# Moving a bias product, eight sums and the last SwiGLU to later or earlier places in the tail of a mixture-of-experts decoder layer

## The chip, the cores and the metric

The kernel runs on one core of one Trainium2 chip. The metric is the device time of one execution in microseconds (us). Engines are named as in the profile: PE (TensorE, matmuls), PEld (its weight loads), DVE (VectorE), ACT (ScalarE), POOL (GpSimd), SP (SyncE, which here issues the large transfers).

## The reference

One post-norm decoder layer over 512 tokens of width 1024: a mixer (a convolution group and dilated attention heads, both projected), a layer norm, a mixture of 32 experts with the top 4 of each token, and a second layer norm. The change lies in the second half:

```python
def reference(...):
    mix = hybrid_mixer(x, ...)
    x = layer_norm(ALPHA * x + mix, ln1_g, ln1_b)
    ffn = moe_ffn(x, router_w, router_b, w_gate, b_gate, w_up, b_up, w_down, b_down)
    return layer_norm(ALPHA * x + ffn, ln2_g, ln2_b)
...
def expert_block(xb, e):                      # one block of tokens that chose expert e
    g = jnp.minimum(xb @ w_gate[e] + b_gate[e], 7.0)
    u = jnp.clip(xb @ w_up[e] + b_up[e], -7.0, 7.0)
    hdn = (u + 1.0) * g * jax.nn.sigmoid(1.702 * g)
    return hdn @ w_down[e] + b_down[e]        # weighted by the gate, added to the token's row
```

## The kernel before, in words

The front (mixer, first norm, routing) fills the first 270 us or so. After it the 32 experts are worked through in an order that is fixed by hand. A *position* is a place in that order, 0 to 31. Tokens of an expert lie in blocks of 32; four blocks make a group. Position 29 has two blocks, positions 30 and 31 have one each, and the one block of position 31 is a group by itself.

For each position `expert` (L1072 to L1128) does on PE four gate/up chunks (L1081 the gate and up biases, L1084 the products), then two down chunks (L1110, L1113). Weights arrive in 2 MB pieces in a ring of seven buffers; a piece is loaded again as soon as PE has read it. After the fourth gate/up chunk comes `swiglu` (L1058): DVE makes `gm` and `um` from PSUM, ACT makes the sigmoid `sg`, DVE multiplies twice and transposes into `hT`, which the down products need. After the down products ACT and DVE copy the result out of PSUM in a high and a low part (`wh`/`yh` L1126, `yl` L1128).

`combine` (L1141) adds finished groups to the tokens' rows `acc`: it makes a one-hot matrix `cg` on DVE (L1146), and then eight times a sum on PE (L1154) and an add on DVE (L1155). Its pieces stand in a list `combs`; `fill` takes the next piece of the oldest entry. `tick(c)` is called after chunk c of a position (0 to 3 gate/up, 4 and 5 down) and calls `fill` as often as `FILLS`, or in the last positions a tuple of its own, says. So `combs` and these numbers set what PE does between chunks. The one-hot is the first piece that `fill` takes of an entry.

`add_bias` (L1325) is an entry of the same list: PE transposes the gates (L1332), DVE copies them (`cg`, L1333), eight PE products with the table of down biases (L1339: 32 rows of the table against 512 columns) are added to `acc` on DVE (L1341), and four PE products with one row (L1346) spread the second norm's gain and bias over the partitions, which ACT copies (L1347).

`overflow` (L1359) is a short entry too: four small PE products and some sixteen small DVE instructions that count blocks over the planned capacity.

Position 31 has its own `tick`: all that is left in `combs` at chunk 0 (`ENDC`), and pieces of `outputs` (L1434) by `ENDO`. A piece of `outputs` works on 128 tokens: statistics on DVE (L1429, L1430), square root (L1431) and scaling (L1446) on ACT, and one step later the gain on DVE (L1449), the bias on POOL (L1451) and the store. Five such pieces make the four row blocks; the sixth (L1457) picks the last group's rows for `last_rows` (L1467), which finishes them when the last down product is there and sends them off with an indirect store (L1563).

Of the kernel before, what the change touches and what calls it, by code (L numbers as in the profile page):

```python
# [18 lines left out]
T, D, H, E, NE, TOPK = 512, 1024, 8, 64, 32, 4  # L19
# [68 lines left out]
LOOK = 2  # L88

FILLS = {False: (0, 0, 0, 3, 0, 0), True: (2, 2, 0, 0, 0, 0)}  # L90
ENDC, ENDO = (99, 99, 99, 99, 0, 0), (0, 3, 2, 6, 0, 0)

PTAPS, GTAPS = (0,) * 4, (8,) * 4
LAGS = dict(V=1.0, bias=-28556.5, c0=30039.3, c1=30045.5, c2=-28570.8, c3=-29890.6, conv0=-29716.5, conv1=30103.6,
# [171 lines left out]
def tile_layer(ctx: ExitStack, tc: tile.TileContext, x, positions, w_in, conv_w, conv_b, conv_ln_g,  # L266
# [792 lines left out]
    def swiglu(st, r, ps):  # L1059
# [10 lines left out]
        V.transpose(st["hT"][:, r].rearrange("p b t -> p (b t)"), um)  # L1070

    def expert(tag, rows, sel, tick, pool=(gd, "gd"), small=lambda: None, keep=False):  # L1072

        ps = [pool[0].tile([128, 2, 256], F32, name=pool[1]) for _ in rows]
        bv = bT.rearrange("p g (h q j) -> p g h q j", h=2, q=4)
        for c in range(4):
            w = got[tag, "gu", c].rearrange("p g k (h q j) -> p k g h q j", h=2, q=4)
            for i, (st, r) in enumerate(rows):
                if c == 0:
                    for q in range(4):  # L1080
                        P.matmul(ps[i][q * 32:(q + 1) * 32], sel[0:96], bv[:, :, :, q], start=True, stop=False)  # L1081
                for k in range(2):
                    for q in range(4):
                        P.matmul(ps[i][q * 32:(q + 1) * 32], st["xT"][:, r, c * 2 + k], w[:, k, :, :, q], start=False,  # L1084
                                 stop=(c == 3 and k == 1))
                if c:
                    small()
                if c == 3:
                    swiglu(st, r, ps[i])
            advance()  # L1090
            tick(c)
# [10 lines left out]
        for c in range(2):  # L1102
            w = got[tag, "dn", c].rearrange("p k (b q c) -> p k q b c", b=4, q=4)
            for u_, (st, r, n) in enumerate(units):
                d = ds_[u_]
                for k in range(4):
                    kw = dict(start=(c == 0 and k == 0), stop=(c == 1 and k == 3))
                    for j in range(4):
                        if n == 2:
                            P.matmul(d[j * 32:(j + 1) * 32], st["hT"][:, r + j % 2, c * 4 + k],  # L1110
                                     w[:, k, 2 * (j // 2):2 * (j // 2) + 2], **kw)
                        else:
                            P.matmul(d[j * 32:(j + 1) * 32, 0:256], st["hT"][:, r, c * 4 + k], w[:, k, j], **kw)  # L1113
            advance()
            tick(4 + c)
# [16 lines left out]
    def place_y(st):  # L1132

        g = st["g"]
        while any(g - 3 in c[1] for c in combs):
            fill()
        if g % 3 not in ys:
            ys[g % 3] = px.tile([128, D], F32R, name="wh" if g % 3 < 2 else "wl")
        st["yh"], st["yl"] = ys[g % 3], mw.tile([128, D], F32R, name="yl", bufs=3)

    def combine(sts):  # L1141

        parts = []
        for st in sts:
            cg = mw.tile([128, T], F32R, name="cg")
            V.tensor_scalar(cg, iota1, st["tk"][:, 0:1], None, op0=OP.is_equal)  # L1146
            parts += [(cg, st[y], st["used"] * 32) for y in ("yh", "yl")]
        yield
        for tt in range(TT):
            for hf in range(2):  # L1150
                c = slice(hf * 512, (hf + 1) * 512)
                ps = cb.tile([128, 512], F32, name="cb")
                for j, (cg, y, n) in enumerate(parts):
                    P.matmul(ps, cg[0:n, tt * 128:(tt + 1) * 128], y[0:n, c], start=(j == 0), stop=(j == len(parts) - 1))  # L1154
                V.tensor_tensor(acc[:, tt, c], acc[:, tt, c], ps, OP.add)  # L1155
                yield
# [33 lines left out]
    GS, combs = {}, []  # L1190

    def begin(i):

        return [(g, s_) for g in range(len(GS), last_group(i) + 1)
                for s_ in [slots(members[g], lambda p, tt: rk1[:, tt, p:p + 1], lambda p, tt: aux[:, tt, p])]
                if next(s_, 0) is None]

    def middle(new):
        for g, s_ in new:
            next(s_)  # L1200

    def finish(new):
        for g, s_ in new:
            GS[g] = dict(next(s_), g=g)

    def ready_x(n):
        for g in range(n + 1):
            if "xT" not in GS[g]:
                xpose(GS[g])

    def fill():
        while combs:
            combs[0][2] -= 1
            if next(combs[0][0], 0) is None:
                return
            combs.pop(0)

    def last_group(i):
        return order[min(i, NE - 1)][1][-1][0]
# [106 lines left out]
    def add_bias():  # L1326

        t = got["last"]
        GT = mw.tile([128, T], F32, name="cg")
        ps = cb.tile([128, 512], F32, name="cb")  # L1330
        for tt in range(TT):
            P.transpose(ps[0:NE, tt * 128:(tt + 1) * 128], Gf[:, tt], ident)  # L1332
        V.tensor_copy(GT[0:NE], ps[0:NE])  # L1333
        bdp = t[0:NE, 0].rearrange("p (b q c) -> p q b c", b=4, q=4)
        yield
        for tt in range(TT):
            for hf in range(2):
                ps = cb.tile([128, 512], F32, name="cb")
                P.matmul(ps, GT[0:NE, tt * 128:(tt + 1) * 128], bdp[:, 2 * hf:2 * hf + 2], start=True, stop=True)  # L1339
                c = slice(hf * 512, (hf + 1) * 512)  # L1340
                V.tensor_tensor(acc[:, tt, c], acc[:, tt, c], ps, OP.add)  # L1341
            yield
        for i in range(4):
            c = slice(i % 2 * 512, (i % 2 + 1) * 512)
            ps = cb.tile([128, 512], F32, name="cb")
            P.matmul(ps, one1, t[0:1, 2 + i // 2, c], start=True, stop=True)  # L1346
            S.activation(t[:, i // 2, c], ps, AF.Copy)  # L1347
            if i % 2:
                yield
# [9 lines left out]
    def overflow():  # L1359

        pcs = cb.tile([128, 512], F32, name="cb")
        for tt in range(TT):
            P.matmul(pcs[:, 0:NE], onesb, mp[:, tt], start=(tt == 0), stop=(tt == TT - 1))
        V.tensor_tensor(ov[:, 0], pcs[:, 0:NE], cap, OP.subtract)
        V.tensor_scalar(ov[:, 1], ov[:, 0], 0.0, None, op0=OP.is_gt)
        for r in range(1, 4):
            V.scalar_tensor_tensor(ov[:, 1], ov[:, 0], 128.0 * r, ov[:, 1], op0=OP.is_gt, op1=OP.add)

        V.tensor_copy(ov[:, 2], ov[:, 1])
        for sft in (1, 2, 4, 8, 16):  # L1370
            V.tensor_copy(ov[:, 3], ov[:, 2])
            V.tensor_tensor(ov[:, 2, sft:NE], ov[:, 3, sft:NE], ov[:, 3, 0:NE - sft], OP.add)
        V.tensor_tensor(ov[:, 1], ov[:, 2], ov[:, 1], OP.subtract)
        V.tensor_copy(nit, ov[0:1, 2, NE - 1:NE])
        yield
# [114 lines left out]
    for i, (p, rows) in enumerate(order):  # L1490
        def tick(c):

            if c == 0:
                middle(new)
            if c == 0 and i == 1:
                combs.append([overflow(), (), 9])
            if c == 1:
                finish(new)
                new.clear()
            if c == 4:  # L1500
                ready_x(last_group(i + 1))
            if c == 5:
                new.extend(begin(i + 1 + LOOK))
            fills = FILLS[len(rows) > 2] if i < NE - 3 else (3, 3, 3, 3, 3, 3)
            if c == 0 and combs and combs[0][1] and combs[0][2] == 9:

                fill()
            if c < 2 and any(g - 3 in k[1] for k in combs for g, r in rows if "yh" not in GS[g]):

                for _ in range(min(3, combs[0][2] - sum(fills[c:]))):  # L1510
                    fill()
            for _ in range(fills[c]):
                fill()

        if i + 1 < NE:
            expert(p, [(GS[g], r) for g, r in rows], selr[:, p] if p else sel0, tick, small=lambda: next(first, 0))
        else:
            break
        if i == LASTC:
            combs.append([add_bias(), (), 9])  # L1520

        ready = order[i + 1][1][0][0] if i + 1 < NE - 1 else ngrp - 1
        while done < ready:
            n = 2 if done < ngrp - 3 else 1
            if done + n > ready:
                break
            combs.append([combine([GS[g] for g in range(done, done + n)]), range(done, done + n), 9])
            done += n

# [61 lines left out]
```

## Time and profile before

| what | us |
|---|---|
| median of 3 runs (lowest, highest) | 1302.81 (1300.8, 1302.96) |
| the profiled execution: its own time | 1306.11 |
| the profiled execution: span of the core | 1304.4 |
| PE busy (share of the span) | 1227.5 (94%) |
| PEld, DVE, ACT, POOL busy | 581.5, 606.1, 280.4, 185.3 |
| moved by the DMA engines | 441.94 MB, 339 GB/s |

The own time is 1.7 us more than the span, which counts from the first to the last instruction. Rows of the trace give times from the start of the span. Time before and time of the profiled execution differ by 3.3 us, so that sums over rows fit the profiled execution and not the median.

### The profile page before, as it was taken

What the parts mean: (1) busy time and instruction counts of PE and PEld (TensorE: products, weight loads), DVE (VectorE), ACT (ScalarE), POOL (GpSimd) and SP (SyncE); (2) the same over time, 40 slices, a digit from 0 to 9 for tenths busy, and PEclk for the clock granted to TensorE, in tenths of its full rate; (3) what the DMA queues carried; (4) which work ended last, traced back from release to release, by engine and by line L of the source; (5) the groups of instructions that cost most, each with busy time, mean ns of one, the idle gap of its engine ahead of it and who ended that gap; (6) DMA issues with size and microseconds to landing.
All of it is one profiled execution on the core that took longest, in us unless ns stands there. A gap on an engine that the chain in (4) does not pass through costs nothing. (4 is left out here: it accounts for less than half of the span.)

```text
span 1304.4 us, 25419 instructions
## 1 busy us (share of the span) xinstructions
PE 1227.5 (94%) x10578; PEld 581.5 (45%) x10578; DVE 606.1 (46%) x1444; ACT 280.4 (21%) x551; POOL 185.3 (14%) x158
## 2 busy tenths in 40 slices
PE   8989999889899999999999899999999999999984
PEld 7767767623233343343344334343435334533332
DVE  6999855743433333342333423344234444324464
ACT  5677782311000010010010001110101110101122
POOL 2854101312011011011001110001101101000002
PEclk9999999879899999999999999999999999999877
DMA  9400324679999999999999999999999999899781
GB/s 293 160 1 1 129 82 173 242 279 377 420 420 419 422 419 421 423 415 419 422 419 420 417 419 422 414 405 419 419 421 410 419 422 419 320 351 368 304 362 68
DMA packets 68658, 441.94 MB, mean 339 GB/s; under 512 B 8279, under 2 KB 16615, under 8 KB 27580
## 3 DMA queue, kind: packets, MB, share of 16 engines
q1 hardware_dynamic: 64748, 429.98, 81.6%
q0 software_dynamic: 3792, 10.29, 2.3%
q8 instruction: 85, 1.39, 0.4%
q14 instruction: 33, 0.27, 0.1%
HBM read 435.99 MB, written 4.33 MB: 338 GB/s over the span
## 5 line engine op out<-in xcount | busy, mean ns | idle before, releaser
L1084 PE MATMUL gd<-wt,xTg 128*32 128x512 f32 x4304 | 505.9, 599 | 7.4 <-DMA wt<-in_exp_w_up_dram 5.1
L1084 PEld LDWEIGHTS gd<-wt,xTg 128*32 128x32 f32 x4304 | 158.2, 111 | 288.2 <-issue 268.4
L1110 PE MATMUL gd<-wt,hT 128*32 128x512 f32 x1472 | 192.4, 602 | 15.3 <-DVE hT L1070 12.6
L1020 POOL DMA_INDIRECT xg<-x1d,idx x78 | 74.4, 954 | 864.7 <-DVE tk L1049 820.8
L1066 ACT ACTIVATE sg<-gm 128x256 f32<-128x256 f32 x78 | 32.5, 417 | 618.1 <-DVE gm L1065 616.0
L1065 DVE TENSOR_SCALAR gm<-gd 128x256 f32<-128x256 f32 x77 | 30.9, 402 | 217.1 <-PE gd L1084 211.0
L1128 DVE TENSOR_TENSOR yl<-gd,wh 32x256 fp32r<-32x256 f32 (+1 forms) x104 | 53.4, 513 | 143.3 <-ACT wh L1126 142.3
L1110 PEld LDWEIGHTS gd<-wt,hT 128*32 128x32 f32 x1472 | 58.6, 111 | 130.3 <-issue 95.7
L1126 ACT ACTIVATE wh<-gd 32x256 fp32r<-32x256 f32 (+1 forms) x104 | 46.8, 450 | 195.0 <-PE gd L1110 135.2
L548 PE MATMUL bk<-wt,wh 128*128 128x512 f32 (+1 forms) x352 | 81.2, 378 | 1.4 <-ACT sg L592 0.7
L1155 DVE TENSOR_TENSOR acc<-acc,cb 128x512 f32<-128x512 f32 x88 | 57.6, 678 | 49.9 <-PE cb L1154 49.7
L1113 PE MATMUL gd<-wt,hT 128*32 128x256 f32 x1056 | 73.0, 392 | 4.6 <-issue 2.5
L1084 PE MATMUL gd<-wb,xTg 128*32 128x512 f32 x624 | 76.7, 593 | 0.0
L548 PEld LDWEIGHTS bk<-wt,wh 128*128 128x128 f32 x352 | 61.1, 188 | 14.7 <-ACT sg L592 1.4
L586 DVE SCALAR_TENSOR_TENSOR bk<-u,cT,bk 128x512 f32<-128x512 f32 x88 | 66.2, 753 | 1.8
L1154 PE MATMUL cb<-yl,cg 128*128 128x512 f32 (+2 forms) x160 | 64.7, 404 | 0.0
L1113 PEld LDWEIGHTS gd<-wt,hT 128*32 128x32 f32 x1056 | 42.4, 113 | 32.6 <-issue 15.5
L1154 PE MATMUL cb<-wh,cg 128*128 128x512 f32 (+2 forms) x112 | 48.2, 431 | 5.9 <-DVE cg L1146 5.9
L1081 PE MATMUL gd<-wl,selr 96*32 96x512 bf16 x296 | 49.1, 385 | 0.0
L548 PE MATMUL bk<-wt,wl 128*128 128x512 f32 (+1 forms) x176 | 41.7, 379 | 2.5 <-DVE wl L539 2.1
L1069 DVE SCALAR_TENSOR_TENSOR um<-um,tk,sg 128x256 f32<-128x256 f32 x78 | 39.7, 509 | 8.9
L1128 DVE TENSOR_TENSOR yl<-gd,wl 64x512 fp32r<-64x512 f32 (+1 forms) x36 | 20.5, 570 | 48.8 <-ACT wl L1126 48.5
(340 smaller groups left out, 1292.6 us busy)
## 6 DMA issues: line engine op xcount, KB each, us to landing
wt<-in_exp_w_gate_dram SPq DMA_DIRECT2D x112, 1024.0 KB
wt<-in_exp_w_up_dram SPq DMA_DIRECT2D x112, 1024.0 KB
wt<-in_exp_w_down_dram SPq DMA_DIRECT2D x52, 2048.0 KB
wb<-in_exp_w_down_dram SPq DMA_DIRECT2D x12, 2048.0 KB
wb<-in_exp_w_gate_dram SPq DMA_DIRECT2D x16, 1024.0 KB
wb<-in_exp_w_up_dram SPq DMA_DIRECT2D x16, 1024.0 KB
wt<-in_w_in_dram SPq DMA_DIRECT2D x3, 2048.0 KB
acc<-in_x_dram SPq DMA_DIRECT2D x8, 512.0 KB
```

Of the source, the lines that this page charges most:

```text
L548: P.matmul(b.t[:, ts], w.t[:, k], xx[:, k, ts], start=(pas == 0 and k == 0), stop=(pas == 2 and k == KT - 1))
L586: op("V", 0.663, (lambda j: lambda e: V.scalar_tensor_tensor(b.t, u[:, c, j:j + T], cT[:, c, j:j + 1], b.t, op0=OP.mult, op1=OP.add))(j), ...
L1020: G.indirect_dma_start(out=xg[:, r], out_offset=None, in_=x1d[:, :], in_offset=bass.IndirectOffsetOnAxis(ap=idx[:, r:r + 1], axis=0))
L1069: V.scalar_tensor_tensor(um, um, st["tk"][:, 8 + r:9 + r], sg, op0=OP.mult, op1=OP.mult)
L1081: P.matmul(ps[i][q * 32:(q + 1) * 32], sel[0:96], bv[:, :, :, q], start=True, stop=False)
L1084: P.matmul(ps[i][q * 32:(q + 1) * 32], st["xT"][:, r, c * 2 + k], w[:, k, :, :, q], start=False, stop=(c == 3 and k == 1))
L1110: P.matmul(d[j * 32:(j + 1) * 32], st["hT"][:, r + j % 2, c * 4 + k], w[:, k, 2 * (j // 2):2 * (j // 2) + 2], **kw)
L1113: P.matmul(d[j * 32:(j + 1) * 32, 0:256], st["hT"][:, r, c * 4 + k], w[:, k, j], **kw)
L1126: S.activation(st["yh"][o], a, AF.Copy)
L1128: V.tensor_tensor(st["yl"][o], a, st["yh"][o].bitcast(F32), OP.subtract)
L1154: P.matmul(ps, cg[0:n, tt * 128:(tt + 1) * 128], y[0:n, c], start=(j == 0), stop=(j == len(parts) - 1))
L1155: V.tensor_tensor(acc[:, tt, c], acc[:, tt, c], ps, OP.add)
```

## The change

A new function `prime` makes the one-hot of the oldest entry of `combs` as soon as that entry is the oldest, at the end of a position or in `fill`, and not at the first `fill` of the next position. `overflow` no longer stands in the list: its pieces are issued together after chunk 4 of position 1. `add_bias` is put in with a count that keeps `prime` off it. The many fills (18 a position) now belong to position 30 alone; position 29 takes `FILLS`, three after chunk 3. In position 31 `ENDO` leaves the third and later pieces of `outputs` but one until after `swiglu`.

```diff
-ENDC, ENDO = (99, 99, 99, 99, 0, 0), (0, 3, 2, 6, 0, 0)
+ENDC, ENDO = (99, 99, 99, 99, 0, 0), (0, 2, 1, 6, 0, 0)
...
     def fill():
         while combs:
+            prime()
             combs[0][2] -= 1
             if next(combs[0][0], 0) is None:
+                if not combs[0][2]:
+                    combs.pop(0)
+                    prime()
                 return
             combs.pop(0)
+
+    def prime():
+
+        if combs and combs[0][2] == 9:
+            combs[0][2] = 8
+            next(combs[0][0])
...
-            if c == 0 and i == 1:
-                combs.append([overflow(), (), 9])
+            if c == 4 and i == 1:
+                for _ in overflow():
+                    pass
...
-            fills = FILLS[len(rows) > 2] if i < NE - 3 else (3, 3, 3, 3, 3, 3)
-            if c == 0 and combs and combs[0][1] and combs[0][2] == 9:
-
-                fill()
+            fills = FILLS[len(rows) > 2] if i < NE - 2 else (2, 3, 3, 3, 3, 2)
...
         if i == LASTC:
-            combs.append([add_bias(), (), 9])
+            combs.append([add_bias(), (), 99])
...
             done += n
+        prime()
```

The instructions of PE and DVE are the same set before and after, but for two more rows on DVE where a run of adds is cut; on ACT a load of the sigmoid's and square root's tables changes place; POOL and SP keep their order. Lines from `prime` on have numbers that are 8 to 10 higher after the change (L1332 becomes L1342, L1339 L1349, L1346 L1356, L1449 L1459).

First place, PE. Before, the bias products stand in position 29 (`x16` is a gate/up chunk of two blocks):

```order
L1332 MATMUL cb<-cst,Gf 32x128 x4
L1339 MATMUL cb<-wt_70,cg 128x512 x2
L1084 MATMUL gd<-wt_1842,xTg 32x512 x16
L1339 MATMUL cb<-wt_70,cg 128x512 x6
L1084 MATMUL gd<-wt_1922,xTg 32x512 x16
L1346 MATMUL cb<-wt_70,one_2115 128x512 x4
L1113 MATMUL gd<-wt_1979,hT 32x256 x32
```

After, they stand in position 30, whose chunks have one block (`x8`); the sums of the last shared group come behind them:

```order
L1084 MATMUL gd<-wt_71,xTg 32x512 x8
L1342 MATMUL cb<-cst,Gf 32x128 x4
L1349 MATMUL cb<-wt_70,cg 128x512 x2
L1084 MATMUL gd<-wt_1789,xTg 32x512 x8
L1349 MATMUL cb<-wt_70,cg 128x512 x6
L1084 MATMUL gd<-wt_1842,xTg 32x512 x8
L1356 MATMUL cb<-wt_70,one_2115 128x512 x4
L1154 MATMUL cb<-wh,cg 128x512
L1154 MATMUL cb<-yl,cg 128x512
L1084 MATMUL gd<-wt_1922,xTg 32x512 x8
```

The products with 32 rows and with one row have kept their order but stand between shorter chunks. In position 29 four sums are left after chunk 0 and twelve stand after chunk 3.

Second place, DVE at the start of position 30. Before:

```order
L1128 TENSOR_TENSOR yl<-gd,wh 32x256 x8
L1146 TENSOR_SCALAR cg<-cst,tk 128x512
L1155 TENSOR_TENSOR acc<-acc,cb 128x512 x8
L1065 TENSOR_SCALAR gm<-gd 128x256
L1067 TENSOR_SCALAR um<-gd 128x256
```

After:

```order
L1128 TENSOR_TENSOR yl<-gd,wh 32x256 x8
L1343 COPY cg<-cb 32x512
L1351 TENSOR_TENSOR acc<-acc,cb 128x512 x8
L1146 TENSOR_SCALAR cg<-cst,tk 128x512
L1155 TENSOR_TENSOR acc<-acc,cb 128x512
L1065 TENSOR_SCALAR gm<-gd 128x256
```

Behind the eight `yl` now stands the copy of the transposed gates, where the one-hot stood.

Third place, DVE in position 31. Before:

```order
L1449 TENSOR_TENSOR yl<-xg,wt_70 128x4x4x64
L1429 BN_STATS lst<-acc 128x6 x2
L1430 BN_AGGR lst<-lst 128x2
L1443 RECIPROCAL lst<-lst 128x1
L1444 TENSOR_SCALAR lst<-lst 128x1
L1449 TENSOR_TENSOR xTg<-xg,wt_70 128x4x4x64
L1449 TENSOR_TENSOR hT<-xg,wt_70 128x4x4x64
L1065 TENSOR_SCALAR gm<-sl 128x256
L1067 TENSOR_SCALAR um<-sl 128x256
L1068 SCALAR_TENSOR_TENSOR um<-um,gm 128x256
L1069 SCALAR_TENSOR_TENSOR um<-um,tk,sg 128x256
L1070 STREAM_TRANSPOSE hT<-um 128x256
```

After:

```order
L1459 TENSOR_TENSOR yl<-xg,wt_70 128x4x4x64
L1065 TENSOR_SCALAR gm<-sl 128x256
L1067 TENSOR_SCALAR um<-sl 128x256
L1068 SCALAR_TENSOR_TENSOR um<-um,gm 128x256
L1069 SCALAR_TENSOR_TENSOR um<-um,tk,sg 128x256
L1070 STREAM_TRANSPOSE hT<-um 128x256
L1439 BN_STATS lst<-acc 128x6 x2
L1440 BN_AGGR lst<-lst 128x2
L1453 RECIPROCAL lst<-lst 128x1
L1454 TENSOR_SCALAR lst<-lst 128x1
L1459 TENSOR_TENSOR xTg<-xg,wt_70 128x4x4x64
L1459 TENSOR_TENSOR hT<-xg,wt_70 128x4x4x64
```

The five instructions of the last SwiGLU have passed the fourth block's statistics and the gains of the third and fourth block.

## Rows read from the trace of the kernel before

**Rows 1.** A window: busy PE, PEld, DVE, ACT, POOL, clock, DMA share, GB/s.
```profile
1200.00:1225.00 25.00, 24.07 (x156) 9.06 (x158) 11.27 (x23) 3.22 (x6) 0.95 (x1) 0.93 0.76 289
```

**Rows 2.** Timeline of PE, 1000 to 1100 us: start, length, work, idle before.
```profile
1068.72 2.50 PE L1084 MATMUL gd<-wt,xTg 128*32 128x512 f32 x16 [2.51 <-DMA wt<-in_exp_w_up_dram]
```

**Rows 3.** Timeline of PE, position 29.
```profile
1192.99 0.50 PE L1154 MATMUL cb<-wh,cg 128*128 128x512 f32 x1
...
1195.96 3.64 PE L1084 MATMUL gd<-wt,xTg 128*32 128x512 f32 x32
...
1200.58 0.60 PE L1332 MATMUL cb<-cst,Gf 128*32 128x128 f32 x4
1202.11 1.98 PE L1339 MATMUL cb<-wt,cg 32*128 32x512 f32 x4 [0.93 <-DVE cg L1333]
1204.02 3.64 PE L1084 MATMUL gd<-wt,xTg 128*32 128x512 f32 x32
1207.59 5.41 PE L1339 MATMUL cb<-wt,cg 32*128 32x512 f32 x12
1212.93 5.34 PE L1084 MATMUL gd<-wt,xTg 128*32 128x512 f32 x32
1218.20 3.69 PE L1346 MATMUL cb<-wt,one 1*128 1x512 f32 x8
```

**Rows 4.** Timeline of PE, positions 30 and 31.
```profile
1228.76 0.40 PE L1081 MATMUL gd<-wl,selr 96*32 96x512 bf16 x4
...
1232.85 0.47 PE L1154 MATMUL cb<-wh,cg 128*128 128x512 f32 x1 [1.98 <-DVE cg L1146]
...
1246.82 3.10 PE L1113 MATMUL gd<-wt,hT 128*32 128x256 f32 x32 [2.47 <-issue]
...
1256.99 0.47 PE L1154 MATMUL cb<-wh,cg 64*128 64x512 f32 x1 [2.88 <-DVE cg L1146]
...
1263.50 7.52 PE L1084 MATMUL sl<-wt,xTg 128*32 128x512 f32 x48
...
1283.87 3.64 PE L1113 MATMUL sl<-wt,hT 128*32 128x256 f32 x32 [5.33 <-issue]
```

**Rows 5.** Windows of 3 us, columns as in rows 1.
```profile
1209.00:1212.00 3.00, 3.00 (x9) 1.29 (x8) 2.49 (x4) 0.00 (x0) 0.00 (x0) 1.00 0.79 309
1212.00:1215.00 3.00, 3.00 (x15) 0.77 (x17) 1.38 (x3) 0.00 (x0) 0.00 (x0) 0.72 0.80 320
...
1233.00:1236.00 3.00, 3.00 (x14) 1.41 (x18) 1.97 (x3) 0.00 (x0) 0.00 (x0) 0.63 1.02 437
...
1248.00:1251.00 3.00, 3.00 (x36) 1.95 (x32) 0.00 (x0) 0.00 (x0) 0.00 (x0) 0.53 1.00 418
...
1260.00:1263.00 3.00, 3.00 (x9) 2.24 (x7) 2.34 (x5) 0.00 (x0) 0.00 (x0) 0.50 0.99 421
```

**Rows 6.** Timeline of DVE, position 1 and positions 30 and 31.
```profile
341.56 1.39 DVE L1128 TENSOR_TENSOR yl<-gd,wh 64x512 fp32r<-64x512 f32 x2 [7.68 <-ACT wh L1126]
...
1228.86 3.46 DVE L1128 TENSOR_TENSOR yl<-gd,wh 32x256 fp32r<-32x256 f32 x8 [8.06 <-ACT wh L1126]
...
1255.54 0.68 DVE L1537 TENSOR_SCALAR ohl<-cst,rk 128x32 f32<-128x32 f32 x4
...
1256.38 0.47 DVE L1146 TENSOR_SCALAR cg<-cst,tk 128x512 fp32r<-128x512 f32 x1
...
1271.98 1.53 DVE L1449 TENSOR_TENSOR yl<-xg,wt 128x1024 f32<-128x1024 f32 x1
...
1278.24 0.42 DVE L1065 TENSOR_SCALAR gm<-sl 128x256 f32<-128x256 f32 x1
...
1279.02 1.78 DVE L1068 SCALAR_TENSOR_TENSOR um<-um,gm 128x256 f32<-128x256 f32 x1
...
1289.86 0.42 DVE L1471 TENSOR_TENSOR wt<-wt,sl 128x256 f32<-128x256 f32 x1 [6.09 <-PE sl L1113]
```

**Rows 7.** Timeline of POOL, position 31.
```profile
1273.66 2.35 POOL L1451 TENSOR_TENSOR yl<-yl,wt 128x1024 f32<-128x1024 f32 x1 [1.22 <-DVE yl L1449]
1277.24 3.29 POOL L1451 TENSOR_TENSOR xTg<-xTg,wt 128x1024 f32<-128x1024 f32 x1 [1.23 <-DVE xTg L1449]
```

## The prediction

> **What bounds the kernel now.** I first asked where time can still be won. Until about 1070 us it is the weights: the timeline of PE shows its last wait for them, 2.51 us at 1068.72 [rows 2]. What is saved ahead of that point is waited for again there, as long as it is no more than 2.51. After it the weights are early: in 1200 to 1225 the DMA engines are busy 0.76 of the time while PE works 24.07 of 25 us [rows 1]. So the tail is bound by PE, and there every wait of PE and every loss of its clock shows in the end. The timeline of PE has these waits: 0.93 for the copy of the gates in position 29 [rows 3], 1.98 and 2.88 for a one-hot, 2.47 and 5.33 for a SwiGLU [rows 4]. [...] From the first row block on the chain runs on DVE: the last SwiGLU starts only at 1278.24, though the last gate/up chunk ended at 1271.02 [rows 4, 6].
>
> **The change part by part.** *One-hots earlier, overflow later.* Before 1068 nothing is won [rows 2]. `overflow` has DVE to itself, since DVE sits idle 7.68 us before the `yl` at 341.56 [rows 6]; moved behind one down chunk, its sixteen instructions still fit at the some 0.2 us that such small ones take, which I estimate as under half of the 0.42 of a `gm` [rows 6]. Without that cover it would cost about 3 us, ahead of 1068. I count 0.
>
> *Position 29* loses the transposes, the wait and the first products (1200.58 to 1204.02, 3.44), the others (1207.59 to 1212.93, 5.34), the one-row products (3.69) and the slow chunk's loss (5.34 less the 3.64 of an undisturbed one, 1.70): **14.2** [rows 3]. Its sums stay, twelve of them behind chunk 3. They take 2.97 (1192.99 to 1195.96) and so cover the SwiGLU, whose wait in position 30 is 2.47 [rows 3, 4]. Position 30 then begins at 1214.6 instead of 1228.76.
>
> *Position 30* gets the bias work: transposes 0.60, eight products 1.98 + 5.41 less the overlap of neighbours, 7.3, one-row products 3.69: 11.6 at the full clock [rows 3]. The wait for the one-hot does not vanish. It becomes one for the copy of the gates, which on DVE stands behind the same eight `yl`: these end 3.56 after the position's start (1228.86 + 3.46 against 1228.76), the copy adds up to 0.93, so PE goes on after 4.4; it has worked 2.1 (1232.85 less the wait of 1.98) and 0.6, and waits 1.7 [rows 3, 4, 6]. That is 0.3 less. Six sums in front of the down products cover half of 2.97, so 1.5, of the 2.47. Together 11.6 - 0.3 - 1.5 = **9.8** more.
>
> *Position 31*: the one-hot passes the four `ohl` and two small instructions (1255.54 to 1256.38, 0.84), and one sum pair, 0.5, now fills part of the wait [rows 6, 4]. So its first sum comes 14.2 - 9.8 + 0.84 + 0.5 = **5.7** earlier than 1256.99, at the same loss of clock.
>
> *The clock* is the open price. Position 30 before has two falls; each costs what the slow chunk lost, 1.7, so 3.4 [rows 3, 5]. After, there lies between the copy and the last gate/up chunk a stretch of 7.3 + 3.7 of 32-row and one-row products, three chunks of 1.9 (half of 3.64 and a little) and a sum pair: 17 us at the full clock [rows 3]. [...] Below: one fall, as after the same products before, 1.7, which is 1.7 better than now. Above: the clock stays down throughout, 17, which is 13.6 worse. The row nearest to it is 1260 to 1263: narrow sums on a busy PE, and the clock stays at 0.50; the three chunks behind them took 7.52 where 5.7 would do, so it comes back late [rows 4, 5]. In position 29 the chunks between the narrow products were 3.64 long, here they are half of that. I take two thirds of the stretch, 11, hence 11 - 3.4 = **7.6** worse. That is the choice on which the number depends most.
>
> [...]
>
> *The last SwiGLU.* On DVE it now follows the second block's gain, which ends at 1273.51 (1271.98 + 1.53) [rows 6]. Not all of 1278.24 - 1273.51 = 4.7 is plain to see: POOL's add of that block runs 1273.66 to 1276.01 [rows 7], and the SwiGLU's first product with two operands in SBUF took 1.78 at 1279.02 and ended at 1280.80, just behind POOL's 1280.53, so it waits for POOL [rows 6, 7]. After, it would start at 1274.3 and end at 1276.3. The other two instructions take about two fifths of 2.47, 1.0, so that `hT` is there at 1277.3 and the down products start at 1277.4 instead of 1283.87, 6.4 earlier [rows 4]. What is late next is the rest of the row blocks, which is now behind the SwiGLU. On DVE it is the 4.7 between 1273.51 and 1278.24, so it would end at 1277.3 + 4.7 = 1282.0; and as the third gain is over before the fourth block is scaled, POOL can take its turn of 2.35 in between, which makes 1284.4 [rows 6, 7]. The down products, if they take the 6.0 they took (1283.87 to 1289.86), end at 1283.4, before that. So the last rows begin at 1284.4 instead of 1289.86: **5.4** earlier [rows 4, 6]. Bounds: 6.4 if the row blocks don't stand in the way, 3.1 if POOL holds DVE for one more turn of 2.35.
>
> *Sum* against the profiled execution: 5.7 - 7.6 + 5.4 = **3.5**. Its own time 1306.11 becomes 1302.6. The median is 3.3 below that execution, and I take the same difference off: **1299.3**.
>
> **The rivals.** *The clock mostly stays up.* Then the stretch costs 1.7 to 7 and the gain, which is 5.7 + 5.4 + 3.4 = 14.5 less the stretch's loss, is 12.8 to 7.5, so 1290.0 to 1295.3. For it: the chunks between are wide and each fall so far ended with such work. Against: the busy PE at 0.50 in 1260 to 1263 [rows 5]. [...]
>
> *Nothing that can be measured*, 1300.3 to 1305.3: the clock costs 12 to 17, and the move of the bias work takes back what the SwiGLU gives. For it: the products of 32 rows and of one row are 11 of 17 us, and at half the clock they last 22. Here the change moves the bias work without its waits going, and only the end gains.
>
> [...]
>
> **How the numbers follow.** What a measurement of this kernel can tell from no change is about 0.2%, 2.6 us: faster is below 1300.2, slower above 1305.4. Chances: forecast, 1296 to 1300.2, 0.36; clock up 0.16; nothing measurable 0.29; slower 0.19. So faster 0.52, same 0.29, slower 0.19. The range leaves out the best part of the first rival and most of the slower one: 1291.5 to 1306.0. The forecast's own range is 1296 to 1302.
>
> **What would show it.** Position 30 starts 14 us earlier and is 10 to 17 us longer. PE waits about 1.7 us there behind L1343's copy. The granted clock between the bias products is near 0.5 for most of the stretch; a clock near 1 is the first rival. The last SwiGLU starts right behind the second block's gain, its first product in SBUF is held by POOL to some 2 us after its start, and the wait of 5.33 before the last down products shrinks below 2. The last rows start behind the fourth block's gain on DVE and not behind PE. The forecast is wrong if the clock holds, or if DVE and POOL hold each other for longer than 5 us in the last position.

## The result, and the profile after

The changed kernel takes **1296.21 us** (median of 5, 1292.78 to 1298.51) against 1302.96 (median of 5 beside it): ratio 0.9933, 95% interval 0.9909 to 0.9958. Twelve more executions on another chip (an experiment below) gave 1300.73 against 1304.76, ratio 0.9967 (0.9946 to 0.9987). So it is faster, by 4 to 7 us; forecast were 3.5 us and 1299.3. The two profiled executions differ by more than that, 1304.4 to 1294.2 in span, and the rows show why.

PE after, from position 29 on (start, length, work, idle before and what ended it):

```profile
1187.59 0.50 PE L1154 MATMUL cb<-wh,cg 128*128 128x512 f32 x1
...
1209.28 0.40 PE L1081 MATMUL gd<-wl,selr 96*32 96x512 bf16 x4
...
1213.59 1.98 PE L1349 MATMUL cb<-wt,cg 32*128 32x512 f32 x4 [1.65 <-DVE cg L1343]
1215.49 1.92 PE L1084 MATMUL gd<-wt,xTg 128*32 128x512 f32 x16
1217.35 7.67 PE L1349 MATMUL cb<-wt,cg 32*128 32x512 f32 x12
1224.95 3.64 PE L1084 MATMUL gd<-wt,xTg 128*32 128x512 f32 x16
1228.52 7.19 PE L1356 MATMUL cb<-wt,one 1*128 1x512 f32 x8
...
1242.86 1.93 PE L1113 MATMUL gd<-wt,hT 128*32 128x256 f32 x32 [0.63 <-DVE hT L1070]
...
1252.26 0.47 PE L1154 MATMUL cb<-wh,cg 64*128 64x512 f32 x1 [1.30 <-DVE cg L1146]
...
1272.39 1.93 PE L1113 MATMUL sl<-wt,hT 128*32 128x256 f32 x32
```

Beside [rows 3, 4]: position 29's first sum starts at 1187.59 instead of 1192.99, so 5.40 us were there before the tail began. Position 29 takes 21.69 (to 1209.28) instead of 35.77. From there to the last group's first sum it is 42.98 instead of 28.23. A gate/up chunk of one block (x16) takes 1.92 at 1215.49, and the next one 3.64 at 1224.95: that is the clock, as the windows after say (the number behind the busy times and ahead of the DMA share is the granted clock):

```profile
1216.00:1219.00 3.00, 3.00 (x20) 1.06 (x13) 0.78 (x2) 0.00 (x0) 0.00 (x0) 1.00 1.01 421
1219.00:1222.00 3.00, 3.00 (x6) 1.21 (x5) 1.92 (x4) 0.00 (x0) 0.00 (x0) 0.72 0.95 404
1222.00:1225.00 3.00, 3.00 (x8) 0.70 (x9) 1.02 (x2) 0.00 (x0) 0.00 (x0) 0.50 0.99 412
...
1237.00:1240.00 3.00, 3.00 (x16) 0.40 (x8) 0.59 (x1) 0.00 (x0) 0.00 (x0) 0.50 0.05 19
1240.00:1243.00 3.00, 2.37 (x14) 1.40 (x14) 2.31 (x6) 0.42 (x1) 0.00 (x0) 0.86 0.48 123
```

In this execution PE is busy 3.00 of 3.00 when the clock falls, and it stands at 0.50 from about 1220 to 1241, through the bias work and one chunk more. A second trace of the same kernel, shown below, has the fall at another place.

DVE and then POOL after, position 31:

```profile
1266.40 1.53 DVE L1459 TENSOR_TENSOR yl<-xg,wt 128x1024 f32<-128x1024 f32 x1
1267.86 0.41 DVE L1065 TENSOR_SCALAR gm<-sl 128x256 f32<-128x256 f32 x1
...
1268.64 2.08 DVE L1068 SCALAR_TENSOR_TENSOR um<-um,gm 128x256 f32<-128x256 f32 x1
...
1275.36 3.28 DVE L1459 TENSOR_TENSOR hT<-xg,wt 128x1024 f32<-128x1024 f32 x1 [0.24 <-ACT xg L1456]
1278.56 0.41 DVE L1481 TENSOR_TENSOR wt<-wt,sl 128x256 f32<-128x256 f32 x1
```

```profile
1268.09 2.35 POOL L1461 TENSOR_TENSOR yl<-yl,wt 128x1024 f32<-128x1024 f32 x1 [1.23 <-DVE yl L1459]
1275.20 2.35 POOL L1461 TENSOR_TENSOR xTg<-xTg,wt 128x1024 f32<-128x1024 f32 x1 [4.76 <-DVE xTg L1459]
...
1285.95 0.89 POOL L1572 DMA_INDIRECT out_dram<-wt,ti  x1 [4.88 <-issue]
```

The SwiGLU starts right behind the second gain, its first product with both operands in SBUF ends just after POOL's add (1268.09 to 1270.44) and takes 2.08 where the median of this line is 0.42, the down products start without a wait at 1272.39, and the last rows start behind the fourth gain, which took 3.28 beside POOL's next add (1275.20 to 1277.55) where the second took 1.53. From the last group's first sum to the last rows it is 26.30 instead of 32.87 [rows 4, 6]. From the last rows to the end it is 15.64 instead of 14.54.

So the 10.2 us between the two profiles are -5.40 ahead of position 29, -14.08 in it, +14.75 to the last group's first sum, -6.57 to the last rows, +1.10 to the end. The tail alone gives 4.8.

### The profile page after: what moved, and what is told of

It is laid out like the page before. It is cut to its first block, busy times and chain, and to the rows that moved or that the text cites. A ratio compares the mean times of both kernels' runs of the same rounds, so it can differ in the third digit from the quotient of the medians.

```text
span 1294.2 us, 25413 instructions
## 1 busy us (share of the span) xinstructions
PE 1227.4 (95%) x10578; PEld 581.2 (45%) x10578; DVE 605.7 (47%) x1444; ACT 280.5 (22%) x551; POOL 184.0 (14%) x158
```

## The experiments

Each was timed beside the kernel before on its chip: the first four on one, the next four on a second, three on a third and the last by itself.

| kernel | us | kernel before | ratio (95%) |
|---|---|---|---|
| the SwiGLU's place alone | 1301.02 | 1304.89 | 0.997 (0.9952 to 0.9987) |
| all but the SwiGLU's place | 1300.06 | 1304.89 | 0.997 (0.9953 to 0.9988) |
| one-hots and overflow alone | 1303.03 | 1304.89 | 0.9984 (0.9963 to 1.0005) |
| after, bias products on 128 rows | 1289.84 | 1304.89 | 0.99 (0.9878 to 0.9921) |
| after, gain and bias spread by DMA | 1293.63 | 1304.76 | 0.9904 (0.9879 to 0.993) |
| after, both | 1287.7 | 1304.76 | 0.9861 (0.9835 to 0.9887) |
| after, bias back in position 29 | 1300.5 | 1304.76 | 0.9968 (0.9955 to 0.9981) |
| after, again | 1300.73 | 1304.76 | 0.9967 (0.9946 to 0.9987) |
| both, bias back in position 29 | 1293.01 | 1302.95 | 0.9912 (0.989 to 0.9934) |
| both, again | 1285.43 | 1302.95 | 0.9856 (0.9833 to 0.988) |
| both, old places of output rows | 1290.19 | 1302.95 | 0.9892 (0.9869 to 0.9915) |
| both, without the last store | 1287.26 | 1306.18 | 0.986 (0.9811 to 0.9909) |

**The parts of the change alone.** The kernel before with the new `ENDO`:

```diff
-ENDC, ENDO = (99, 99, 99, 99, 0, 0), (0, 3, 2, 6, 0, 0)
+ENDC, ENDO = (99, 99, 99, 99, 0, 0), (0, 2, 1, 6, 0, 0)
```

> The kernel before with the order of the output pieces in position 31 alone changed, so that the last SwiGLU passes the third and fourth block. If it is worth what the prediction's sum gave, about 5.4 us less than before, 1297.5; in its profile the last down products start at most 2 us after PE's warm-up matmuls, and all ahead of the second block's gain is as before. If the row blocks merely take the place of the SwiGLU at the end, within 1.5 us of before.

The changed kernel with the old `ENDO`, the same line the other way round:

> The changed kernel with the old order of output pieces in position 31, so that only the move of the bias work, the sums and the one-hots is left. By the prediction's sum (5.7 - 7.6 for the tail, nothing ahead of it) 1.9 us slower than before, 1304.9; if waits ahead of the tail count after all, or the clock holds more often than not, 1.4 us or more faster than before, 1301.5 or less, which with e1 would add up to the change's 6.75.

The changed kernel with the old `ENDO` and the old fills, so that of the change only the earlier one-hots and the place of `overflow` are left:

```diff
-            fills = FILLS[len(rows) > 2] if i < NE - 2 else (2, 3, 3, 3, 3, 2)
+            fills = FILLS[len(rows) > 2] if i < NE - 3 else (3, 3, 3, 3, 3, 3)
```

> The kernel before with one-hots made early and overflow out of the list, the bias work left in position 29 and the old order of output pieces. By the theory that waits ahead of 1068 us are made good by the weights, only the tail's waits count: 1.98 and 0.84 go and with the first its fall of the clock, 2.8 to 4.5 less than before, 1298.5 to 1300.2, with position 29 starting within 1 us of before. By the rival that each wait of PE counts, two more waits of 1.0 go and position 29 starts 2 us or more earlier, 5 to 6.5 less, 1296.5 to 1298.

Measured: 3.9, 4.8 and 1.9 us less than before. The first two are together 0.6% by their ratios, where the change itself gave 0.67% and 0.33%; with some 0.2% of noise on each, that fits, but says no more. The second is a miss: without the SwiGLU's place the prediction's sum gave a loss of 1.9 us, and 4.8 were gained. The third is not told from zero. In its trace the wait of 1.98 in position 30 stayed where I had expected it to go, since DVE still has the eight `yl` ahead of the one-hot, and 2.88 became 2.07.

**The clock: wide against narrow products.** The bias products over 128 rows instead of 32: the table is loaded four times, and the transposed gates get 96 rows of zeros from POOL. Number, columns and results of the products stay the same.

```diff
-        SP.dma_start(t[0:NE, 0], exp_b_down[0])
+        for r in range(4):
+            SP.dma_start(t[r * NE:(r + 1) * NE, 0], exp_b_down[0])
...
-        V.tensor_copy(GT[0:NE], ps[0:NE])
-        bdp = t[0:NE, 0].rearrange("p (b q c) -> p q b c", b=4, q=4)
+        for r in range(4):
+            (V.tensor_copy(GT[0:NE], ps[0:NE]) if r == 0 else G.memset(GT[r * NE:(r + 1) * NE], 0.0))
+        bdp = t[:, 0].rearrange("p (b q c) -> p q b c", b=4, q=4)
...
-                P.matmul(ps, GT[0:NE, tt * 128:(tt + 1) * 128], bdp[:, 2 * hf:2 * hf + 2], start=True, stop=True)
+                P.matmul(ps, GT[:, tt * 128:(tt + 1) * 128], bdp[:, 2 * hf:2 * hf + 2], start=True, stop=True)
```

> The changed kernel with the bias products over 128 rows instead of 32 (the table is loaded four times, the gates' other rows are zero), which are as long at the same clock. If narrow products on a busy PE take the clock down, it stays up through them and falls at most once behind the one-row products: the 9.9 us that the bias stretch lost to the clock shrink to 2 to 5, 5 to 8 us less than the changed kernel, 1288 to 1291. [...]

PE of this kernel, and its windows:

```profile
1213.66 1.95 PE L1351 MATMUL cb<-wt,cg 128*128 128x512 f32 x4 [1.74 <-DVE cg L1345]
...
1217.40 5.42 PE L1351 MATMUL cb<-wt,cg 128*128 128x512 f32 x12
1222.75 1.92 PE L1084 MATMUL gd<-wt,xTg 128*32 128x512 f32 x16
1224.60 4.34 PE L1358 MATMUL cb<-wt,one 1*128 1x512 f32 x8
...
1230.03 3.64 PE L1084 MATMUL gd<-wt,xTg 128*32 128x512 f32 x16
```

```profile
1222.00:1225.00 3.00, 3.00 (x19) 0.71 (x18) 1.77 (x3) 0.00 (x0) 0.00 (x0) 1.00 1.00 415
1225.00:1228.00 3.00, 3.00 (x8) 1.11 (x6) 0.00 (x0) 1.72 (x3) 0.00 (x0) 0.92 1.02 423
1228.00:1231.00 3.00, 3.00 (x12) 0.82 (x14) 0.69 (x1) 0.67 (x2) 0.00 (x0) 0.50 1.01 421
```

The wait ahead of the products is the same (1.74 against 1.65), they run at 1.00 throughout, and the clock falls only in the one-row products, again on a busy PE, some 14 us after that wait. The 1289.84 lies in the range that was expected if narrow products matter. The next edit takes the one-row products away: the transfer spreads gain and bias, and the table moves to another slot.

```diff
-        SP.dma_start(t[0:NE, 0], exp_b_down[0])
+        SP.dma_start(t[0:NE, 2], exp_b_down[0])
...
-            SP.dma_start(t[0:1, 2 + i], bass.AP(tensor=a.tensor, offset=a.offset, ap=[[0, 1], [1, D]]))
+            SP.dma_start(t[:, i], bass.AP(tensor=a.tensor, offset=a.offset, ap=[[0, 128], [1, D]]))
...
-        bdp = t[0:NE, 0].rearrange("p (b q c) -> p q b c", b=4, q=4)
+        bdp = t[0:NE, 2].rearrange("p (b q c) -> p q b c", b=4, q=4)
...
-        for i in range(4):
-            c = slice(i % 2 * 512, (i % 2 + 1) * 512)
-            ps = cb.tile([128, 512], F32, name="cb")
-            P.matmul(ps, one1, t[0:1, 2 + i // 2, c], start=True, stop=True)
-            S.activation(t[:, i // 2, c], ps, AF.Copy)
-            if i % 2:
-                yield
```

> The changed kernel, with the second norm's gain and bias loaded onto all 128 partitions by the transfer (table of expert biases in slot 2 instead), and without the four one-row products and ACT's four copies. In the changed kernel these four took 7.19 us, at a granted clock of 0.50 from about 1220.4 to 1240.7. Theory (narrow products on a busy PE take the clock down, and the stretch lasts some 17 to 20 us from its fall): the products on 32 rows still bring the fall, the stretch stays as long and covers other work, so only 3.7 us (their time at the full clock) is saved, 1292.5 us. If the one-row products prolong the stretch, up to 7.2 us, 1289 us. Rival (only waits take the clock down): 3.7 us as well, but the stretch begins where a wait is, not behind the products on 32 rows. Rival (loading 1 MB more on the queue delays weights): no gain or a loss.

> Both: bias products over 128 rows (the table loaded four times, 96 rows of the gates' transposes zero) and gain and bias spread by the transfer. Theory (narrow products take the clock down): no narrow product is left in this stage until the first sums, the clock stays at 1.0 through position 30, about 10 us of the changed kernel's loss to the clock and 3.7 us of one-row products are saved: against 1289.8 us of the wide products alone some 4 to 5 us less, 1285 us. Rival (only waits take the clock down, the wide products' gain was chance): 1292.5 us, as without them.

> The changed kernel once more, beside the three others on one chip: 1296.2 us and a ratio of 0.9933 to before if the chip does not matter; where its granted clock falls behind the products on 32 rows again (1220 us of its span), the fall belongs to the kernel and not to chance.

PE with the spread alone:

```profile
1216.90 2.79 PE L1349 MATMUL cb<-wt,cg 32*128 32x512 f32 x4 [1.66 <-DVE cg L1343]
1219.62 3.64 PE L1084 MATMUL gd<-wt,xTg 128*32 128x512 f32 x16
1223.19 10.61 PE L1349 MATMUL cb<-wt,cg 32*128 32x512 f32 x12
...
1239.38 1.92 PE L1084 MATMUL gd<-wt,xTg 128*32 128x512 f32 x16
```

PE and windows with both, in the second run of that kernel:

```profile
1215.12 1.96 PE L1351 MATMUL cb<-wt,cg 128*128 128x512 f32 x4 [1.75 <-DVE cg L1345]
...
1218.86 5.42 PE L1351 MATMUL cb<-wt,cg 128*128 128x512 f32 x12
1224.21 1.92 PE L1084 MATMUL gd<-wt,xTg 128*32 128x512 f32 x16
...
1240.94 0.46 PE L1154 MATMUL cb<-wh,cg 64*128 64x512 f32 x1 [2.10 <-DVE cg L1146]
```

```profile
1222.00:1225.00 3.00, 3.00 (x14) 1.02 (x16) 2.49 (x5) 0.00 (x0) 0.00 (x0) 1.00 0.93 391
...
1237.00:1240.00 3.00, 1.84 (x20) 0.33 (x12) 1.40 (x4) 2.91 (x6) 0.00 (x0) 1.00 1.02 421
1240.00:1243.00 3.00, 2.06 (x7) 1.53 (x8) 2.87 (x11) 0.48 (x1) 0.00 (x0) 0.86 1.04 426
1243.00:1246.00 3.00, 3.00 (x9) 2.30 (x7) 2.56 (x4) 0.00 (x0) 0.00 (x0) 0.50 1.02 434
```

With the spread alone the fall is there again (10.61 is nearly twice 5.41), but it comes about 1 us behind the wait of 1.66. A stretch that begins at a wait was the sign put on record for the rival in which only waits count. The second trace of the changed kernel, whose fall had been expected at about 1220 again, looks alike (PE, and windows of 3 us):

```profile
1213.75 3.48 PE L1349 MATMUL cb<-wt,cg 32*128 32x512 f32 x4 [1.65 <-DVE cg L1343]
1217.16 3.64 PE L1084 MATMUL gd<-wt,xTg 128*32 128x512 f32 x16
1220.73 7.23 PE L1349 MATMUL cb<-wt,cg 32*128 32x512 f32 x12
```

```profile
1211.00:1214.00 3.00, 1.35 (x13) 0.56 (x6) 2.61 (x6) 0.23 (x1) 0.00 (x0) 1.00 1.05 445
1214.00:1217.00 3.00, 3.00 (x4) 0.69 (x3) 0.69 (x1) 0.00 (x0) 0.00 (x0) 0.51 1.01 431
...
1220.00:1223.00 3.00, 3.00 (x9) 1.11 (x6) 0.87 (x2) 0.00 (x0) 0.00 (x0) 0.85 0.96 407
```

Here the clock falls within half a microsecond of the wait, is back at about 1221, and falls twice more. So the stretch of 17 to 20 us that was put on record is in two traces (about 1220 to 1241, and with the spread alone 1218 to 1238 by the lengths of its rows) and not in this one, and the place of the fall does not tell its cause. The pair of edits does: the same wait (1.65 or 1.66, with the zeros 1.74 or 1.75) stands ahead of the bias products in nine traces. All four with 32 rows lose the clock during the bias products (the row of twelve takes 7.67, 10.61 and 7.23 in those shown), and all five with 128 rows keep it at 1.00 through them (5.42 in the two shown). In these traces a wait of this length did not bring the fall by itself; with narrow products behind it the clock fell each time. No run has the 32-row products in position 30 without a wait ahead. In [rows 3, 5], with the products in position 29, the fall comes 11 us after a wait of 0.93.

With both edits position 30 is at 1.00 from end to end. The first fall comes in the last group's sums, which have 64 rows and also follow a wait of 2.10, so either can be its cause.

Both together are 13.0 us faster than the changed kernel beside them (1287.7, where 1285 had been expected); the 3.7 of the one-row products and the clock's 9.7 (below) make 13.4. The spread alone gave 7.1 by the medians, where 3.7 had been expected, but 2 to 3 by the traces from position 30's first product to the end (81.92, against 84.92 and 84.06 in the two of the changed kernel). Whether it is worth 3.7 or 7 is not settled.

**The bias work in its old place.** First the changed kernel with the old fills (the line shown above), then the same edit in the kernel with both.

> The changed kernel with the old table of fills: bias products and last sums stay in the third last place; one-hots ahead, overflow's place and the last SwiGLU ahead of most output rows as changed. If the steps add up (the SwiGLU alone gave a ratio of 0.997, the one-hots alone 0.9984), the ratio to before is 0.9954, 1298.9 us, and the bias's move is worth about 2.5 us. If the move of the bias costs time by the clock (predicted: 14.2 us saved in the third last place, 9.8 and 7.6 us given back), about 1293 to 1296 us, no slower than the changed kernel.

> The version with wide bias products and gain and bias spread by the transfer, with the old table of fills: bias products and last sums back in the third last place. It asks what the move alone is worth when the clock stays up. Theory (the prediction's terms for positions 29 and 30 without the clock): the move takes 10.5 us out of position 29 (14.2 less 3.7 of one-row products that are gone) and puts 6.1 into position 30 (9.8 less 3.7), so without the move the kernel is 4.4 us slower than the one with it (4.9 more with the earlier first sum), about 1292 us at 1287.7 for the other. Rival (moving work within a PE-bound stretch changes nothing): the same time, 1287.7 us.

> The version with wide bias products and gain and bias spread by the transfer, once more beside the two others: ratio 0.986 to before as on the other chip, with position 30 at a granted clock near 1.0 up to its last chunk.

The changed kernel was no faster than with the bias work in its old place: 1300.73 and 1300.5, where 1298.9 at most had been expected for the latter. The same pair with the old `ENDO`, in the first table rows, says 3.0 us for the move (1300.06 against 1303.03). So with narrow products the move is worth 0 to 3 us. In the versions in which the bias work leaves the clock up, the old place is 7.6 us slower (1293.01 against 1285.43). Of these some 2 are the edit's own: PE waits there 2.11 for POOL's zeros where [rows 3] have 0.93, and 0.70 and 0.25 for a SwiGLU that the one-row products used to cover. So the move is worth 5 to 6 us without the narrow products, and they took most of that back. PE with the old place, narrow products:

```profile
1202.45 1.98 PE L1349 MATMUL cb<-wt,cg 32*128 32x512 f32 x4 [0.93 <-DVE cg L1343]
1204.36 5.34 PE L1084 MATMUL gd<-wt,xTg 128*32 128x512 f32 x32
...
1220.23 5.14 PE L1356 MATMUL cb<-wt,one 1*128 1x512 f32 x8
1225.31 5.54 PE L1113 MATMUL gd<-wt,hT 128*32 128x256 f32 x64
```

Against [rows 3] three more pieces are slow here, the three rows with 5.34, 5.14 and 5.54: position 29 lasted 40.8 us (from 1193.34 on) and not 35.8. Of four traces with the narrow products in the old place two show 35.8 and two 40.8. And PE with the old place, wide products:

```profile
1202.00 1.98 PE L1351 MATMUL cb<-wt,cg 128*128 128x512 f32 x4 [2.11 <-POOL cg L1345]
...
1241.02 3.44 PE L1113 MATMUL gd<-wt,hT 128*32 128x256 f32 x32 [2.46 <-issue]
```

The last row shows the other kind of fall: behind the wait of 2.46, after wide work only, the down products take 3.44 where 1.93 is their time, and the window from 1241 to 1244 shows 0.55. But not every wait is followed by one: in the same trace PE waits 1.98 for a one-hot in position 30, as in [rows 4], and the clock stays at 1.00, while it falls behind that wait in all four traces with the narrow products in position 29 (0.63 in [rows 5]).

**The last position.** The kernel with both edits (wide bias products, gain and bias spread by the transfer), and the old `ENDO`:

> The same version with the old places of the output rows, so that the last SwiGLU comes behind four more steps of them again. Theory (prediction's term of 5.4 us for the last rows): 5.4 us slower than the version with both, about 1293 us. Rival (the gain of the SwiGLU's move hung on the slow clock before it): less than 2.6 us slower.

The last rows on DVE of this kernel wait for PE again, as in [rows 6]:

```profile
1272.32 0.42 DVE L1476 TENSOR_TENSOR wt<-wt,sl 128x256 f32<-128x256 f32 x1 [5.33 <-PE sl L1113]
```

It is 4.8 us slower than the version with both (5.4 had been expected): the SwiGLU's place is worth nearly the same with the clock up. Four traces with the old places have 31.4 to 32.9 us from the last group's first sum to the last rows, nine with the new ones 25.9 to 27.0; between the means that is 5.7. But from the last rows to the end the four take 14.5 us and the nine 15.4 to 17.3, on the mean 1.8 more, so that 3.9 are left of the 5.7. Part of this lies between DVE's memset behind the last rows and POOL's store of them: 1.3 us in the four, 1.3 to 3.5 in the nine. The last edit asks why, by leaving out a store; its output lacks these 128 rows:

```diff
-                SP.dma_start(out[0, (tt - 1) * 128:tt * 128, :], o)
+                if tt < TT:
+                    SP.dma_start(out[0, (tt - 1) * 128:tt * 128, :], o)
```

> The version with wide bias products and spread gain and bias, without the store of the fourth row block (its 128 rows are left out of the output). In all nine traces with the last SwiGLU ahead of the output rows, 1.3 to 3.5 us lie between DVE's last memset and POOL's store of the last rows, and 1.3 in all four with the old order; the last store is issued 2.3 to 3.3 us before that memset in the former, 11 to 12 us before it in the latter. Theory (the waits in the block of the empty loop end with that store's landing): 1.3 us, where the two traces of this version have 3.24 and 3.53. Rival (code loading or another wait): 3 us or more, as with the store.

DVE, then POOL of this kernel:

```profile
1278.26 0.06 DVE L1386 MEMSET ctr<- 128x1 f32 x1
```

```profile
1279.81 0.89 POOL L1568 DMA_INDIRECT out_dram<-wt,ti  x1 [4.27 <-issue]
```

From the memset to the store it is 1.55 where the two traces of this version with the store have 3.24 and 3.53. This is one trace, four of the nine with the store have 1.3 to 1.8 as well, and the medians (1287.26, beside another run of the kernel before) can't show 1.7 us. So it is not shown that the store is the cause. It points there: in the five traces with 3.1 to 3.5 the last store is issued 2.3 to 3.0 us before the memset, in the other four 3.1 to 3.3, and in the old order 11 to 12.

## Why the prediction was right, and where its sizes were off

**The sign and the range** were right. The tail alone gave 4.8 us in the profile, for 3.5 forecast. That the two are so close is in part luck: the clock cost 1.3 less than forecast, the stretch to the last rows gave 1.2 more (6.57 for 5.4), and the way from the last rows to the end took back 1.1 that the sum did not have. Over all traces the bias work's move was better than forecast and the SwiGLU's place worse, and the two errors partly offset each other.

*One-hots earlier: 0.* Not told from 0 (ratio 0.9984, interval over 1), but the reason given for it is not borne out. The waits for a one-hot of 1.00 at 763.62 and 1.01 at 992.79 in the trace before are gone in the trace after. The wait for the weights that ends at 1068.72 [rows 2] is 2.90 there instead of 2.51, but it is 2.90 as well with the SwiGLU's place alone, where the two waits are as before. So no trace shows that it takes back what they give. The 5.40 us by which the profile after is ahead at position 29 can't be put down to this or to any other part of the change. The kernel with the SwiGLU's place alone has the program of before up to there and is further ahead (1186.24), and one that has every edit of the change is behind (1193.11, the first run with both edits of the bias work). Of the 5.40, 2.6 are there at 367 us of the trace before, behind a stretch with another granted clock (0.86 before, 0.91 after, 0.88 with the SwiGLU's place alone); the rest comes between 732 and 1078 us. Window of the kernel before and of after:

```profile
250.00:350.00 100.00, 84.23 (x784) 30.79 (x788) 46.63 (x173) 14.95 (x24) 18.85 (x18) 0.86 0.89 347
```

```profile
250.00:350.00 100.00, 84.19 (x818) 30.85 (x818) 48.42 (x178) 15.52 (x25) 18.98 (x18) 0.91 0.91 355
```

*Position 29 loses 14.2:* measured 14.08, in these two traces. Of the four traces with the old place two would have given 5 more, so the term depends on which execution it is taken from, and I gave it no bounds. From position 29's first sum to the last group's first sum the four take 63.2 to 69.1 us, 66.1 on the mean, and the three traces with all the narrow products in position 30 take 64.2 to 64.7. So the move gives 1.6 us on the mean where the sum has 5.7 - 7.6, a loss of 1.9. With this the kernel without the SwiGLU's place is faster than before, as measured, and not slower.

*Position 30 gets 9.8:* right at the same clock. The wait behind the copy of the gates is 1.65 for 1.7 forecast, the SwiGLU's 0.63 for 1.0.

*The clock, 7.6 worse:* a loss of the kind forecast, a size of 6.3. The losses after are 2.26 (7.67 for 5.41), 3.50 (7.19 for 3.69), twice 1.72 (3.64 for 1.92) and 0.5 in the sums around, 9.7 in all where I took 11. Against the 3.4 of before that is 6.3. A piece at 0.50 took about twice its time (7.19 for 3.69, 3.64 for 1.92), so 17 us at 0.50 throughout would have lost some 17, my upper bound. The second trace of the changed kernel has three shorter falls, the first right behind the wait, and the same loss of 9.7. The step that the forecast rested on, that narrow products take the clock down, is shown by the wide products; that they do it without a wait ahead is not. In the bias work the waits alone do not account for the falls: behind those of 1.74 and 1.75, ahead of wide products, the clock stayed at 1.00, and behind those of 1.65 and 1.66, ahead of narrow ones, it fell. The fall behind the wait of 2.46 (0.55) came after wide work only, so not every fall here has narrow products just ahead of it.

*The last SwiGLU, 5.4:* right up to the last rows, 5.7 between the means of the traces, with POOL's two holds where they were put (2.08, and 3.28 where I had feared one more turn). What I missed stands behind it: from the last rows to the end it takes 1.8 us more on the mean, a term that the sum put at nothing. In five of nine traces 1.8 to 2.2 us of it pass before POOL's store of the last rows, perhaps because the store before it is now late. That leaves 3.9; by medians the place was worth 3.9 and 4.8.

The rival "nothing measurable" was wrong for the whole, but right for one half: what the SwiGLU gave stayed, and the bias work's move alone gave little: nothing on one chip (1300.73 against 1300.5), 3.0 us on another (1300.06 against 1303.03).

## What to carry to other kernels

Price a move of narrow matmuls (few rows) at the clock that they may cost (9.7 us here), and first ask whether they can be made wide: 96 rows of zeros cost nothing on PE here (5.42 us for 5.41), and together with the removal of the one-row products they were worth 13.0 us on top of the 4.0 that the change gave on the same chip. The best version, wide bias products with gain and bias spread by the transfer, ran at 1285.43 and 1287.7 us, ratio 0.9856 (0.9833 to 0.988) and 0.9861 (0.9835 to 0.9887). Take a term from several executions where a clock is in it, and split two profiles by stage before crediting a difference to the edit: here half of it lay ahead of the tail and could not be put down to the edit. When a last piece of work is pulled ahead, look at what it was pulled ahead of: here the last store came later, and the end took 1.8 us longer.

## What was not expected of the hardware

The same instructions in the same order lose the clock at different places from one execution to the next: the row of twelve 32-row products took 7.67 in one trace of the changed kernel and 7.23 in the second, where the row of four was slow as well (3.48 for 1.98). In the version without one-row products they took 10.61, about twice 5.41, and the row of four ahead of them was slow from about 1 us after the wait (2.79 for 1.98). Position 29 with narrow products lasted 35.8 or 40.8 us. That the loss in position 30 was 9.7 both times, wherever it began, was not expected either. In the version with wide bias products the clock went from 1.00 (1222 to 1225) to 0.50 (1228 to 1231) in the products with one row, without a wait just ahead. Not so in [rows 3]: there they ran at the full clock (3.69), and the windows behind them, to 1229, show 1.00.
